# Two mixers of an encoder: the pooled branch's window sums from VectorE to GpSimd

## Chip, cores and metric

The kernel runs on one core of a Trainium2 chip, in one launch. The metric is the device time in microseconds (us) of one execution; less is better. Weights and inputs come from HBM. All arithmetic is float32, and the large products are made from a high and a low part of each operand (float32r), three matmuls for one.

## The reference, cut to what matters

The model has an attention layer, a recurrent layer and then two layers of feed-forward, hybrid mixer, feed-forward. The change touches the hybrid mixer alone, which runs twice (layer 0 and 1). With S = 256 positions and D = 1024:

```python
def causal_pool_mixer(u, pool_w, pool_scale):          # u: [1, 256, 512], 4 groups of 128
    ...
    for g, w in enumerate((2, 4, 8, 16)):              # a window of its own for each group
        lo = jnp.maximum(pos - w, 0)
        window_sum = cs[:, 1:, g] - cs[:, lo, g]
        means.append(window_sum / (pos - lo)[None, :, None])
    mixed = jnp.einsum('bsgc,gcd->bsgd', jnp.stack(means, axis=2) - ug, pool_w)
    return mixed.reshape(b_, s_, 512) * pool_scale

def hybrid_mixer(...):
    u_pool, q_pre, f_pre, i_in, og, gates = jnp.split(h @ w_in, splits, axis=-1)
    pool_out = causal_pool_mixer(u_pool, pool_w, pool_scale)
    ...                                                # a gated linear recurrence over 4 heads: o
    hgrn_out = o * hgrn_norm * jax.nn.silu(og)
    g = jax.nn.sigmoid(gates).reshape(b_, s_, 2, D)
    merged = g[:, :, 0] * (pool_out @ w_pool_proj) + g[:, :, 1] * (hgrn_out @ w_hgrn_proj)
    return merged @ w_out
```

## The kernel before, in words

Channels lie on the 128 partitions and positions along the columns, so a group of the pooled branch is a tile of 128x256. TensorE makes all products. A weight arrives by DMA in a tile `raw`; ScalarE rounds it to `hi` and VectorE makes the rest, `lo` = `raw` - `hi` (`cut`, line 427); activations are split in the same way (`split`, line 473).

The order of the instructions on every engine is written by a planner in the kernel itself. Side work is written as generators (`spawn`), and the planner keeps a modelled clock for each engine (`Clock`, `Engine`). A generator is resumed at the point where TensorE's modelled clock has passed the end of what it last issued, so an instruction's place in TensorE's queue is where the planner expects its operands. For GpSimd its price is 0.1 us and 0.0026 us a column, and 0.12 us for a signal from one instruction to one that needs its result. On the chip each engine takes its queue in order and waits on semaphores.

`hybrid` (line 1472) first makes the products of `h` with `w_in` in pairs of 128 output channels (`pair`), in the order f, q, v, u, og, gates; `scaled` takes each out of PSUM. Beside the later pairs runs `memory`, the linear recurrence: eight levels, each with exponentials on ScalarE (`xx`), two additions (`xx`, `lf`) and two products (`kq`) on VectorE and small matmuls on TensorE. The first six levels' matmuls go into three PSUM tiles `lv`, which `diagonal` masks into `pr` (six levels of 256 columns) and adds up with one reduction. After the levels `memory` normalises the result `ob` and splits it into `hh`, `hl`, the operands of the linear branch.

`pooled` (line 1683) makes the pooled branch. It waits for `u` and for "pool free", which `memory` puts after its last level, since the sums use the buffers of the scan (`lf`, `kk_`, and `ex` as `pd`). Each of four rounds doubles the window for all the groups that are left (one addition, one copy of the first columns), finishes one group (product with 1/count on the first 16 columns, subtraction, scaling with subtraction on the rest), and has TensorE multiply it with `pw`; the result is split into `ph`, `pl`, which the trace calls `hph` and `hpl`. `pd` appears there as `xx`, `up_` with a number behind it.

Then come eight branch products. Each is a pooled half (12 matmuls, from `ph`, `pl`) and a linear half (12 matmuls, from `hh`, `hl`) in one PSUM tile; `merge` multiplies them with the gates. The product with `w_out` follows. PSUM has eight tiles: two `acc` and six `m`; a product takes an `m` where no `acc` is free.

Of the kernel before, what the change touches and what calls it, by code (L numbers as in the profile page):

```python
# [12 lines left out]
ALU = mybir.AluOpType  # L13
AX = mybir.AxisListType
PSUM = bass.MemoryType.PSUM

P = 128
D = 1024
NM = 16
S = 256  # L20
# [99 lines left out]
class Clock:  # L120
# [9 lines left out]
    def range(self, ap):  # L130
        dims = list(ap.ap)
        per = dims[0][0] or 1 << 30
        lo = ap.offset % per
        return ap.tensor.name, lo, lo + 1 + sum((n - 1) * abs(s) for s, n in dims[1:])
# [92 lines left out]
class Builder:  # L227
# [1244 lines left out]
    def hybrid(self, layer, gen):  # L1472
        nc, a = self.nc, self.a
        tt, ts, stt, act, mm = self.tt, self.ts, self.stt, self.act, self.mm
# [5 lines left out]
        hy = self.pool(st, "hy")  # L1480
# [3 lines left out]
        cols = slice(0, S)  # L1484
        big = lambda tag: self.t(hy, [P, H, S], tag)
        fl = lambda t: t.rearrange("p h t -> p (h t)")
        hyb = self.hyb
# [15 lines left out]
        fz, qs = big("fz"), big("qz")  # L1503
        vt = self.t(hy, [P, 2, 512], "vt")
        lf, kk_, w0 = big("lf"), big("kk"), big("w0")
        xx = self.t(hy, [P, 2 * H, S], "xx")
        ex, x2 = xx[:, :H, :], xx[:, H:, :]
        at0 = self.t(hy, [P, H, S], "at0")
        at1 = self.t(hy, [P, H, P], "at1")
        up_, gz = big("up_"), self.t(hy, [P, 16, S], "gz")  # L1510
        ob, og, pd = fz, w0, ex
        pw = self.t(hy, [P, 4, P], "pw")
        pr = self.t(hy, [P, 6, S], "pr")
        hh, hl = self.t(hy, [P, H, S], "hh", F32R), self.t(hy, [P, H, S], "hl", F32R)
        ph, pl = self.t(hy, [P, H, S], "hph", F32R), self.t(hy, [P, H, S], "hpl", F32R)

        def memory():
# [46 lines left out]
            def diagonal():  # L1564

                msk = hyb[:, H_AT["level"][0]:H_AT["level"][0] + 192].rearrange("p (l c) -> p l c", l=6)
                for j in range(3):
                    tt(out=pr[:, 2 * j:2 * j + 2, :].rearrange("p l (g c) -> p l g c", c=32),
                       in0=lv[j].rearrange("p (l g c) -> p l g c", l=2, c=32),
                       in1=msk[:, 2 * j:2 * j + 2, :].unsqueeze(2).to_broadcast([P, 2, 8, 32]), op=ALU.mult)  # L1570
                    self.drop(lv[j])
                    yield "dve"
                blk = (yield from self.grab("work"))[:, :S]
                nc.vector.tensor_reduce(out=blk, in_=pr.rearrange("p l n -> p n l"), axis=AX.X, op=ALU.add)
                yield
                bv = blk.rearrange("p (h j c) -> p h j c", h=H, c=32)
                for q in range(4):
                    p0 = 32 * q
                    nc.scalar.copy(out=at0[p0:p0 + 32, :, p0:p0 + 32], in_=bv[p0:p0 + 32, :, 0, :])
                    nc.scalar.copy(out=at1[p0:p0 + 32, :, p0:p0 + 32], in_=bv[p0:p0 + 32, :, 1, :])  # L1580
                self.put("diag", gen)
# [4 lines left out]
            for i in range(8):  # L1586
# [3 lines left out]
                last = lambda v, h=h: v[:, :, h - 1:h].to_broadcast([P, N // (2 * h), h])  # L1590
# [14 lines left out]
                if i < 5:  # L1605
                    small(i + 1, kq, kq)
                    if i == 4:
                        self.keep(*lv)
                        self.spawn(diagonal(), *lv)
                        up = yield from self.grab("m", 2)  # L1610
                elif i < 7:
                    for hd in range(H):
                        for t0 in range(0, S, 2 * h):
                            j, p0 = t0 // P, t0 % P
                            mm(out=up[j][p0:p0 + h, hd * P + p0 + h:hd * P + p0 + 2 * h],
                               lhsT=kq[:, hd, t0:t0 + h], rhs=kq[:, hd, t0 + h:t0 + 2 * h], start=True, stop=True)
                    yield
                    for j, dst in ((0, at0), (1, at1)):
                        uv = up[j].rearrange("p (h t) -> p h t", h=H)
                        for p0 in range(0, P, 2 * h):  # L1620
                            nc.vector.tensor_copy(out=dst[p0:p0 + h, :, p0 + h:p0 + 2 * h], in_=uv[p0:p0 + h, :, p0 + h:p0 + 2 * h])
                else:
                    ps = up.pop()
                    for hd in range(H):
                        mm(out=ps[:, hd * P:(hd + 1) * P], lhsT=kq[:, hd, 0:P], rhs=kq[:, hd, P:S], start=True, stop=True)
                    yield
                    nc.scalar.copy(out=at0[:, :, P:S], in_=ps.rearrange("p (h t) -> p h t", h=H))
                    self.drop(ps, *up)
                self.drop(kq)
            self.put("pool free", gen)  # L1630
            yield from self.wait("diag", gen)
            yield from self.wait("v", gen)
            sq = yield from self.grab("kq")
            for i in range(2):
                ps = yield from self.grab("m")
# [30 lines left out]
            for i in range(2):  # L1666
                ps = yield from self.grab("m")
# [13 lines left out]
                    self.put("hh", gen, hd)  # L1681

        def pooled():
            yield from self.wait("u", gen, 2)
            yield from self.wait("pool free", gen)
            cur = up_
            for g in range(4):
                wd = 1 << g
                dst = (lf, kk_)[g % 2]
                tt(out=dst[:, g:, wd:], in0=cur[:, g:, wd:], in1=cur[:, g:, 0:S - wd], op=ALU.add)  # L1690
                nc.vector.tensor_copy(out=dst[:, g:, 0:wd], in_=cur[:, g:, 0:wd])
                yield
                i0 = H_AT["inv"][0] + g * NM
                tt(out=pd[:, g, 0:NM], in0=dst[:, g, 0:NM], in1=hyb[:, i0:i0 + NM], op=ALU.mult)
                tt(out=pd[:, g, 0:NM], in0=pd[:, g, 0:NM], in1=up_[:, g, 0:NM], op=ALU.subtract)
                stt(out=pd[:, g, NM:], in0=dst[:, g, NM:], scalar=0.5 / wd, in1=up_[:, g, NM:], op0=ALU.mult, op1=ALU.subtract)
                cur = dst
                yield
                ps = yield from self.grab("m")
                mm(out=ps[:, :S], lhsT=pw[:, g, :], rhs=pd[:, g, :], start=True, stop=True)  # L1700
                yield
                self.split(ps[:, :S], ph[:, g, :], pl[:, g, :], self.v("pool_scale", layer * 4 + g))
                self.drop(ps)
                self.put("ph", gen, g)
# [18 lines left out]
        self.spawn(first(), *pp)  # L1723
        pair(2, fz[:, 2:4, :], ("f2", gen, 0))
        self.spawn(memory())
        for e in (4, 6):
            pair(e, qs[:, e - 4:e - 2, :], ("q", gen, e - 4))
        pv = self.take("acc", 2)
        for c in range(2):
            for half in range(2):  # L1730
                w = self.piece("hi", layer * 2 + c, half)
# [9 lines left out]
        self.drop(*pv)  # L1741
        self.put("v", gen)
        self.spawn(pooled())
        self.spawn(output_gate())
        for c in HYBRID:
            e = 2 * c
            if e < 12:
                dst, name, e0 = up_, "u", 8
            elif e < 16:
                dst, name, e0 = og, "g", 12  # L1750
                self.need("og free", gen)
            else:
                dst, name, e0 = gz, "z", 16
# [14 lines left out]
        def merge(e, ps):  # L1768
            yield from self.wait("gz", gen)
            m0, m1 = [t[:, :S] for t in (yield from self.grab("work", 2))]  # L1770
            stt(out=m0, in0=gz[:, e, :], scalar=1.0, in1=ps[:, 0:S], op0=ALU.add, op1=ALU.mult)
            stt(out=m1, in0=gz[:, 8 + e, :], scalar=1.0, in1=ps[:, S:2 * S], op0=ALU.add, op1=ALU.mult)
            yield
            tt(out=m0, in0=m0, in1=m1, op=ALU.add)
            self.split(m0, mh[:, e, :], ml[:, e, :], 0.5)
            self.put("m", gen, e)

        for e in range(8):
            w = self.piece("wph", layer * 4 + e // 2, e % 2)
            ps = self.take("acc")  # L1780
            self.run(self.prod(ps[:, 0:S], w, e % 2 * 1024, ph, pl, range(4), cols, key=("ph", gen))
                     + self.prod(ps[:, S:2 * S], w, e % 2 * 1024 + 512, hh, hl, range(4), cols, key=("hh", gen), last=True))
            self.spawn(merge(e, ps), ps)
        self.prep(S)

        def residual(d, ps):
# [5 lines left out]
        for d0, n in ((0, 4), (4, 1), (5, 1), (6, 1), (7, 1)):  # L1792
            ps, steps = [], []
            for d in range(d0, d0 + n):
                w = self.piece("hout", layer * 4 + d // 2, d % 2)
# [215 lines left out]
```

## Time and profile before

| | |
|---|---|
| median of 3 runs | 1526.24 us (1525.52 to 1527.98) |
| profiled execution | 1526.28 us, of it 1524.49 us from the first to the last instruction |
| TensorE (PE) busy | 1492.8 us, 98% |
| VectorE (DVE) busy | 1116.3 us, 73% |
| ScalarE (ACT) busy | 903.1 us, 59% |
| GpSimd (POOL) busy | 26.2 us, 2%, 68 instructions |
| mean granted TensorE clock | 0.996 |

Layer 0's mixer lies at about 645 to 800 us of the span, layer 1's at 1170 to 1345 us. In the profile PE is TensorE, DVE VectorE, ACT ScalarE, POOL GpSimd; a granted clock of 1.00 is 2.4 GHz and 0.50 is 1.2 GHz. Almost every instruction bears the line of the planner's helper (L181), so rows are told apart by tile: `lo<-raw,hi` reads `raw` and `hi` and writes `lo`.

### The profile page before, as it was taken

To read this page: it belongs to the slowest core of one execution; us is meant where nothing else is said; L and a number is where in the kernel's file an instruction comes from. 1 tells how busy PE (TensorE), PEld (TensorE's weight loads), DVE (VectorE), ACT (ScalarE), POOL (GpSimd) and SP (SyncE) were. 2 spreads that over 40 slices of the span, in tenths; PEclk is the share of its full clock that TensorE was granted. 3 is DMA by queue.
4 is the path that set the end of the run, shared out by engine and by line. 5 is a ranking of instruction groups with operands and counts; after the bars stand their busy time and mean duration, and the time that the engine had idled before them with its cause. 6 is when DMAs were issued, how large, how long until landed. Compare 5 with 4: busy or idle time off the path is not lost.

```text
span 1524.5 us, 31049 instructions
## 1 busy us (share of the span) xinstructions
PE 1492.8 (98%) x12950; PEld 1458.6 (96%) x12950; DVE 1116.3 (73%) x1882; ACT 903.1 (59%) x1435; POOL 26.2 (2%) x68
## 2 busy tenths in 40 slices
PE   8999999999999999999999999999999998999998
PEld 8988899999999999999999999999999998999998
DVE  6977775689997666669887666666666788877754
ACT  7666654689966654575555554455455754555553
POOL 1000000000000000000000000000000000000000
PEclk9999999999999999999999999999999999999999
DMA  6422224544455555554545655655556444456553
GB/s 239 158 90 84 83 84 141 201 159 168 138 170 190 198 201 172 207 175 146 180 164 186 225 184 177 207 193 197 184 176 227 166 140 138 166 184 223 185 171 123
DMA packets 42492, 259.12 MB, mean 170 GB/s; under 512 B 4840, under 2 KB 6256, under 8 KB 18416
## 3 DMA queue, kind: packets, MB, share of 16 engines
q1 hardware_dynamic: 40624, 251.90, 47.6%
q10 hardware_dynamic: 1728, 5.24, 1.0%
q8 instruction: 101, 1.65, 0.4%
q14 instruction: 39, 0.32, 0.1%
HBM read 256.07 MB, written 1.05 MB: 169 GB/s over the span
## 4 chain that ended last, share of the span: by engine, by line
PE 60%; issue 26%; DVE 8%; ACT 4%; DMA 1%; POOL 1%; SPq 0%; ACTq 0%; DVEq 0%; POOLq 0%
PE acc L181 45%; PE m L181 14%; DVE lo L181 3%; ACT hi L181 2%; DVE big L181 2%; DVE kq L181 1%; ACT w L181 1%; ACT L181 1%; ACT xx L181 1%; DVE xx L181 0%; DVE lf L181 0%; DVE work L181 0%; DMA raw<-in_hin_dram 0%; DMA raw<-in_hi_dram 0%; POOL col L181 0%
## 5 line engine op out<-in xcount | busy, mean ns | idle before, releaser
L181 DVE TENSOR_TENSOR lo<-raw,hi 128x1024 fp32r<-128x1024 f32 (+3 forms) x520 | 582.6, 1129 | 248.0 <-ACT hi L181 243.6
L181 ACT ACTIVATE hi<-raw 128x1024 fp32r<-128x1024 f32 (+3 forms) x520 | 501.5, 980 | 286.7 <-PE acc L181 187.9
L181 PE MATMUL acc<-xh,hi 128*128 128x256 f32 (+1 forms) x2096 | 588.4, 281 | 5.6 <-ACT hi L181 5.6
L181 PE MATMUL acc<-xl,hi 128*128 128x256 f32 (+1 forms) x2096 | 589.0, 281 | 0.0
L181 PE MATMUL acc<-xh,lo 128*128 128x256 f32 (+1 forms) x2096 | 587.4, 280 | 0.0
L181 PEld LDWEIGHTS acc<-xh,hi 128*128 128x128 f32 x2096 | 395.0, 188 | 7.0 <-ACT hi L181 5.6
L181 PEld LDWEIGHTS acc<-xl,hi 128*128 128x128 f32 x2096 | 395.1, 188 | 1.3
L181 PEld LDWEIGHTS acc<-xh,lo 128*128 128x128 f32 x2096 | 394.7, 188 | 1.3 <-DVE lo L181 0.2
L181 PE MATMUL acc<-ph,lo 128*128 128x256 f32 x704 | 194.3, 276 | 0.0
L181 PE MATMUL acc<-ph,hi 128*128 128x256 f32 x704 | 194.3, 276 | 0.0
L181 PE MATMUL acc<-pl,hi 128*128 128x256 f32 x704 | 194.3, 276 | 0.0
L181 PEld LDWEIGHTS acc<-ph,lo 128*128 128x128 f32 x704 | 132.2, 188 | 0.0
L181 PEld LDWEIGHTS acc<-ph,hi 128*128 128x128 f32 x704 | 132.2, 188 | 0.0
L181 PEld LDWEIGHTS acc<-pl,hi 128*128 128x128 f32 x704 | 132.2, 188 | 0.0
L181 PE MATMUL m<-xh,lo 128*128 128x256 f32 (+1 forms) x336 | 95.7, 285 | 0.0
L181 PE MATMUL m<-xl,hi 128*128 128x256 f32 (+1 forms) x336 | 95.5, 284 | 0.0
L181 PE MATMUL m<-xh,hi 128*128 128x256 f32 (+1 forms) x336 | 95.2, 283 | 0.0
L181 DVE TENSOR_TENSOR work<-acc,spread 128x256 f32<-128x256 f32 (+1 forms) x108 | 46.0, 427 | 36.5 <-PE acc L181 32.3
L181 ACT ACTIVATE work<-work 128x256 f32<-128x256 f32 (+2 forms) x92 | 37.4, 408 | 51.7 <-DVE work L181 51.4
L181 PEld LDWEIGHTS m<-xh,hi 128*128 128x128 f32 x336 | 63.7, 190 | 0.2
L181 PEld LDWEIGHTS m<-xh,lo 128*128 128x128 f32 x336 | 63.6, 189 | 0.3
L181 PEld LDWEIGHTS m<-xl,hi 128*128 128x128 f32 x336 | 63.6, 189 | 0.1
(359 smaller groups left out, 2242.2 us busy)
## 6 DMA issues: line engine op xcount, KB each, us to landing
raw<-in_ffn_gu_dram SPq DMA_DIRECT2D x88, 1024.0 KB, 4.9
raw<-in_ffn_dn_dram SPq DMA_DIRECT2D x64, 704.0 KB, 4.1
raw<-in_hin_dram SPq DMA_DIRECT2D x32, 1024.0 KB, 4.9
raw<-in_oin_dram SPq DMA_DIRECT2D x16, 1024.0 KB, 4.9
raw<-in_ein_dram SPq DMA_DIRECT2D x12, 1024.0 KB, 4.8
raw<-in_eout_dram SPq DMA_DIRECT2D x8, 1024.0 KB, 4.9
raw<-in_oout_dram SPq DMA_DIRECT2D x8, 1024.0 KB, 4.9
raw<-in_wph_dram SPq DMA_DIRECT2D x8, 1024.0 KB, 4.9
```

What stands on the lines that cost most here:

```text
L181: r = f(*args, **kw)
```

## The change

Three things in `hybrid`. The window sums go from VectorE to GpSimd: group by group, each from `u` anew, in two tiles `win` of 128x256 of their own, and as soon as `u` is there; "pool free" is gone. A group g makes g+1 additions with as many small copies, a small product, a scaling and a subtraction, then the matmul with `pw` and the split as before. The masked levels are added up pair by pair as they come, so that `pr` has four levels instead of six and the reduction is an addition of two. The pooled halves of the first four branch products are issued before the four linear halves; the other four products are as before.

```diff
-        ob, og, pd = fz, w0, ex
+        ob, og = fz, w0
-        pr = self.t(hy, [P, 6, S], "pr")
+        pr = self.t(hy, [P, 4, S], "pr")
+        win = [self.t(hy, [P, S], f"win{i}") for i in range(2)]
...
                 for j in range(3):
-                    tt(out=pr[:, 2 * j:2 * j + 2, :].rearrange("p l (g c) -> p l g c", c=32),
+                    to = pr[:, 2:4, :] if j else pr[:, 0:2, :]
+                    tt(out=to.rearrange("p l (g c) -> p l g c", c=32),
...
+                    if j:
+                        tt(out=pr[:, 0:2, :], in0=pr[:, 0:2, :], in1=to, op=ALU.add)
                     yield "dve"
                 blk = (yield from self.grab("work"))[:, :S]
-                nc.vector.tensor_reduce(out=blk, in_=pr.rearrange("p l n -> p n l"), axis=AX.X, op=ALU.add)
+                tt(out=blk, in0=pr[:, 0, :], in1=pr[:, 1, :], op=ALU.add)
...
-            self.put("pool free", gen)
...
         def pooled():
+            g_ = nc.gpsimd
             yield from self.wait("u", gen, 2)
-            yield from self.wait("pool free", gen)
-            cur = up_
             for g in range(4):
-                wd = 1 << g
-                dst = (lf, kk_)[g % 2]
-                tt(out=dst[:, g:, wd:], in0=cur[:, g:, wd:], in1=cur[:, g:, 0:S - wd], op=ALU.add)
-                nc.vector.tensor_copy(out=dst[:, g:, 0:wd], in_=cur[:, g:, 0:wd])
-                yield
+                u = cur = up_[:, g, :]
+                for n in range(g + 1):
+                    wd, dst = 1 << n, win[n % 2]
+                    g_.tensor_tensor(out=dst[:, wd:], in0=cur[:, wd:], in1=cur[:, 0:S - wd], op=ALU.add)
+                    g_.tensor_copy(out=dst[:, 0:wd], in_=cur[:, 0:wd])
+                    cur = dst
                 i0 = H_AT["inv"][0] + g * NM
-                tt(out=pd[:, g, 0:NM], in0=dst[:, g, 0:NM], in1=hyb[:, i0:i0 + NM], op=ALU.mult)
-                tt(out=pd[:, g, 0:NM], in0=pd[:, g, 0:NM], in1=up_[:, g, 0:NM], op=ALU.subtract)
-                stt(out=pd[:, g, NM:], in0=dst[:, g, NM:], scalar=0.5 / wd, in1=up_[:, g, NM:], op0=ALU.mult, op1=ALU.subtract)
-                cur = dst
+                g_.tensor_tensor(out=cur[:, 0:NM], in0=cur[:, 0:NM], in1=hyb[:, i0:i0 + NM], op=ALU.mult)
+                g_.tensor_scalar(out=cur[:, NM:], in0=cur[:, NM:], scalar1=0.5 / wd, scalar2=None, op0=ALU.mult)
+                g_.tensor_tensor(out=cur, in0=cur, in1=u, op=ALU.subtract)
                 yield
                 ps = yield from self.grab("m")
-                mm(out=ps[:, :S], lhsT=pw[:, g, :], rhs=pd[:, g, :], start=True, stop=True)
+                mm(out=ps[:, :S], lhsT=pw[:, g, :], rhs=cur, start=True, stop=True)
...
-        for e in range(8):
-            w = self.piece("wph", layer * 4 + e // 2, e % 2)
-            ps = self.take("acc")
-            self.run(self.prod(ps[:, 0:S], w, e % 2 * 1024, ph, pl, range(4), cols, key=("ph", gen))
-                     + self.prod(ps[:, S:2 * S], w, e % 2 * 1024 + 512, hh, hl, range(4), cols, key=("hh", gen), last=True))
-            self.spawn(merge(e, ps), ps)
+        for e0, n in ((0, 4), (4, 1), (5, 1), (6, 1), (7, 1)):
+            pooled_, linear, ps = [], [], []
+            for e in range(e0, e0 + n):
+                w = self.piece("wph", layer * 4 + e // 2, e % 2)
+                ps.append(self.take("acc"))
+                pooled_ += self.prod(ps[-1][:, 0:S], w, e % 2 * 1024, ph, pl, range(4), cols, key=("ph", gen))
+                linear += self.prod(ps[-1][:, S:2 * S], w, e % 2 * 1024 + 512, hh, hl, range(4), cols, key=("hh", gen), last=True)
+            self.run(pooled_ + linear)
+            for i in range(n):
+                self.spawn(merge(e0 + i, ps[i]), ps[i])
```

## Rows read from the trace of the kernel before

**Rows 1.** Busy us by engine in stretches: PE, PEld, DVE, ACT, POOL, granted clock, DMA
```profile
690.00:711.00 21.00, 19.49 (x332) 18.74 (x319) 19.88 (x27) 11.77 (x16) 0.00 (x0) 1.00 0.45 153
711.00:760.00 49.00, 48.59 (x418) 47.80 (x418) 41.63 (x70) 26.61 (x40) 1.64 (x1) 1.00 0.46 154
1210.00:1231.00 21.00, 19.04 (x335) 18.33 (x336) 16.82 (x22) 15.64 (x19) 0.00 (x0) 1.00 0.54 197
1285.00:1291.00 6.00, 2.06 (x8) 1.06 (x8) 5.55 (x15) 1.74 (x4) 0.00 (x0) 0.97 0.22 91
1291.00:1294.00 3.00, 3.00 (x15) 3.00 (x16) 0.69 (x1) 1.99 (x3) 0.00 (x0) 0.50 0.00 0
```

**Rows 2.** Chain of work that ended last, both mixers: start us, us, what
```profile
691.65 1.23 DVE lo L181
...
705.05 1.22 DVE kq L181 x2
...
707.01 12.80 PE acc L181 x111
...
740.29 0.43 PE m L181 x2
...
1252.18 2.93 DVE work L181
```

**Rows 3.** TensorE in order of time, 1284 to 1294 us: start, us, [idle before <-releaser]
```profile
1284.93 0.28 PE L181 MATMUL acc<-hph,hi 128*128 128x256 f32 x1
...
1286.37 0.39 PE L181 MATMUL acc<-hpl,hi 128*128 128x256 f32 x1 [1.16 <-DVE hpl L181]
...
1288.76 0.70 PE L181 MATMUL m<-xx,pw 128*128 128x256 f32 x2 [1.90 <-DVE xx L181]
...
1291.32 0.41 PE L181 MATMUL acc<-hh,hi 128*128 128x256 f32 x1
...
1293.88 0.39 PE L181 MATMUL acc<-hph,hi 128*128 128x256 f32 x1
```

**Rows 4.** VectorE's groups, 1268 to 1292 us: busy us, mean ns | idle before
```profile
L181 DVE SCALAR_TENSOR_TENSOR hpl<-m,vec,hph 128x256 fp32r<-128x256 f32 x4 | 1.9, 478 | 0.8 <-ACT hph L181 0.8
...
L181 DVE TENSOR_TENSOR lf<-up__12257 128x1020 f32<-128x1020 f32 x1 | 1.2, 1216 | 0.0
...
L181 DVE SCALAR_TENSOR_TENSOR xx<-lf,up__12257 128x240 f32<-128x240 f32 x2 | 0.8, 402 | 0.0
```

**Rows 5.** VectorE in order of time, the last part of the linear operand
```profile
1291.03 0.69 DVE L181 TENSOR_TENSOR hl<-fz,hh 128x512 fp32r<-128x512 f32 x1 [0.36 <-ACT hh L181]
```

**Rows 6.** GpSimd and VectorE in order of time, where both work
```profile
36.85 1.11 POOL L181 COPY kz<-kpe 64x272 f32<-64x272 f32 x2 [13.75 <-DVE kpe L181]
37.04 0.65 DVE L181 TENSOR_TENSOR mq<-mq,work 128x272 f32<-128x272 f32 x1
39.48 0.44 DVE L181 TENSOR_TENSOR mq<-mq,work 128x272 f32<-128x272 f32 x1
...
467.07 0.70 POOL L181 TENSOR_TENSOR col<-mx,half 128x2 f32<-128x2 f32 x1 [143.36 <-DVE mx L181]
...
814.68 1.22 DVE L181 TENSOR_TENSOR lo<-raw,hi 128x1024 fp32r<-128x1024 f32 x1
814.85 1.61 POOL L181 TENSOR_TENSOR col<-mx,half 128x2 f32<-128x2 f32 x1 [75.67 <-DVE mx L181]
...
990.01 0.48 DVE L181 TENSOR_SCALAR work<-cst,col 128x128 f32<-128x128 f32 x2 [0.88 <-POOL col L181]
...
1171.59 1.10 DVE L181 TENSOR_SCALAR work<-cst,col 128x128 f32<-128x128 f32 x2
1171.59 0.95 POOL L181 MEMSET at<- 128x1024 f32 x1
```

**Rows 7.** Writers of `u`, layer 0 and 1: ns min/median/max, first and last start
```profile
L181 DVE TENSOR_TENSOR up__6512<-acc,spread x2: 682/683/684, 682.8 to 689.3; 128x512 f32<-128x512 f32 x2
...
L181 DVE TENSOR_TENSOR up__12257<-acc,spread x2: 685/686/687, 1205.4 to 1209.4; 128x512 f32<-128x512 f32 x2
```

## Prediction

> **What bounds the kernel now.** I read the busy time by stretches first. In both mixers there are two kinds of stretch. From 690 to 711 us and from 1210 to 1231 us the queues of VectorE and ScalarE set the pace: VectorE is busy 19.88 and 16.82 of 21 us, TensorE only 19.49 and 19.04, so TensorE idles 1.5 and 2.0 us. From 711 to 760 us TensorE sets it (48.59 of 49 us) [rows 1]. The chain of work that ended last says the same: a level of the scan runs through the weight cut `lo` (1.23 us) and the products `kq` (0.61 us each) on VectorE, and only after 706 us does it pass to TensorE, 111 matmuls in 12.80 us, 0.115 us each [rows 2].
>
> The third kind is the end of the second mixer. From 1285 to 1291 us TensorE has 8 matmuls and VectorE is full; from 1291 to 1294 us the granted clock is 0.50, the lower of TensorE's two levels, 1.2 GHz, after that idle stretch [rows 1]. TensorE stands in the first branch product, waiting for `hpl`, then for the last pooled group, which VectorE makes between other work [rows 3]. Layer 0 has no such hole [rows 1].
>
> **The tail of the second mixer: -6.5 us.** From 1284.93 to 1291.32 us are 6.4 us [rows 3]; in them lie six matmuls of 0.115 and one pool product of 0.43 us [rows 2], 1.1 us, so 5.3 us are lost. The twelve matmuls from 1291.32 to 1293.88 us take 2.56 us at the lower clock [rows 3] instead of 12 x 0.115 = 1.4: 1.2 more. With the pooled branch finished early and 48 pooled matmuls (5.5 us) in front of the first linear half, no wait for `hph` is left. What is late next is `hl`: its last part ends at 1291.72 us [rows 5]. In front of it after 1282 us VectorE loses two `hpl` (0.48 each) and two subtractions (0.40 each) [rows 4], at least 1.8 us, so it comes at 1289.9 us. TensorE would ask for it after 45 more pooled matmuls and six linear ones, 5.9 us past 1284.93 less the pool product of 0.43, at 1290.4 us. So the cover holds; if VectorE were not relieved at all it would cost 1.3 us (bounds -5.2 and -6.5).
>
> **VectorE's window additions, gone.** The first takes 1.22 us, each final subtraction 0.40 [rows 4], some 7 us in a layer with the three smaller additions and the small columns. I book nothing for them beyond the tail: in layer 0 they lie in the stretch where TensorE is full. The work that hides them is TensorE's own; nothing is to be had there.
>
> **The masked levels: -0.4 us.** A reduction of 2.93 us [rows 2] goes; two additions of 128x512 (0.61, as `kq`) and one half as wide (0.4, as the subtraction [rows 4]) come. In layer 1 the reduction lies on the chain: 2.93 - 1.6 = -1.3; I take -1.1. In layer 0 it lies behind the last level, whose matmuls end the chain's VectorE part [rows 2], while the first addition stands in front of that level: +0.7. Bounds -1.3 (nothing lost in layer 0) and +0.7 (nothing gained in layer 1).
>
> **Pool products moved: -3.2 us.** Four of 0.43 us a layer [rows 2] leave the stretches that TensorE fills and go where it idles 1.5 and 2.0 us [rows 1]: -1.7 in layer 0, -1.5 in layer 1 (the tail is counted above). Bounds -3.4 and 0.
>
> **Their splits, moved too: +2.9 us.** Four `hpl` of 0.48 us a layer [rows 4] now stand in VectorE's queue ahead of the cuts and level products that TensorE waits for. Three of four come before the last level of layer 0 (1.4), four at a busy share of 16.82 / 21 in layer 1 (1.5). Bounds 0 and 3.8. ScalarE's `hph` beside them, of like size, hide in its 9 and 5 idle us of each stretch [rows 1]. The DMA of `pw` is issued at the layer's start as before, on the same queue.
>
> **GpSimd beside VectorE: +7.8 us.** A group g makes g+1 steps of an addition and a small copy, then a small product, a scaling and a subtraction: in a layer 14 wide operations with two inputs, 4 wide ones with one, 14 small ones, 32 in all. They start when `u` is written, at 690.0 and 1210.1 us [rows 7], exactly where VectorE sets the pace. No row shows a wide addition on GpSimd. What rows do show is that the two engines hold each other up. A two-column power takes 0.70 us alone and 1.61 us when VectorE has just begun a cut [rows 6]. The other way round, a copy of 272 columns stretches a VectorE product of 0.44 to 0.65 us, by 0.21, and a GpSimd memset beside it makes a pair of scalings take 1.10 instead of 0.48 us, 0.62 more [rows 6]. An addition reads twice what the copy reads: I take 2 x 0.21 = 0.42 us held, 0.21 for a one-input operation, 0.05 for a small one: 14 x 0.42 + 4 x 0.21 + 14 x 0.05 = 7.4 us a layer. Three levels of two cuts and four level products, 3 x (2 x 1.23 + 4 x 0.61) = 14.7 of 21 us [rows 2], read two operands in SBUF, as that stretched product did; so 0.7 of the holds meet one: 5.2 us. VectorE's idle time of 1.1 and 4.2 us [rows 1] absorbs half of itself, since the rest lies inside the chain: 4.7 + 3.1 = 7.8 us. Bounds: 0 (all holds fall into gaps) and 2 x (18 x 0.62 + 14 x 0.1) = 25 us (0.1 for a small one is twice my value; no row has one). A power and a clearing for the linear branch stand behind these on GpSimd's queue, but come 40 us later.
>
> The Trainium skill (SBUF — State Buffer, section "Who interferes with whom") says that whichever of the two engines starts first gets the shared port pair for its whole instruction and the other fully blocks; the rows agree in direction. It speaks against this change. So does the Trainium skill's GPSIMD Engine Reference (section 3.1, "Elementwise — side-by-side cycle accounting"): 2.6 cycles per element for an addition at 1.2 GHz, an estimated 0.55 us for 256 columns, which no row here shows. With 0.55 held instead of 0.42, the sum would be 2.5 us higher.
>
> **The sum** is -6.5 - 0.4 - 3.2 + 2.9 + 7.8 = +0.6 us on the profiled execution's 1526.28 us (span 1524.49 and 1.8 around it; the median of the three runs is 1526.24): **1526.9, say 1527 us**. So a sure gain at one place is paid for by a likely loss at two. The four products' open banks cost nothing that I can see: eight banks, and the merges follow the linear halves as before.
>
> **The rivals.** (A) GpSimd fits into VectorE's gaps, holds 2 us a layer or less: 1526.3 - 6.5 - 0.4 - 3.2 + 2.9 + 0 to 4 = 1519 to 1523 us. For it: 1.1 and 4.2 us of VectorE idle, and operands from PSUM in part of its work; against it: the chain runs through VectorE there. Chance 0.33.
>
> (B) Slower: TensorE stops at the pool products. TensorE takes its queue in order, and each pool product stands where the kernel's own planner expects the group's end. With each of 32 operations waiting for a VectorE operation under way, half of 0.61 to 1.23 us [rows 2] at 0.7, 0.3 us, the chain is 10 us longer than alone. Alone it takes between 18 x 0.53 + 14 x 0.1 = 10.9 us (the copies of [rows 6]: two in 1.11) and twice that for two inputs, 18 us. The planner allows some 19 us: at its price of 0.1 us and 0.0026 us a column, with 0.12 us for each signal, the groups take 2.9, 3.9, 4.8 and 5.8 us, with the products between them. Where the chain passes that, TensorE waits, and behind the waiting product stand the pairs and the level products. From 3 us past the plan this decides; at 4 to 8 us a layer on top of the forecast, of which up to 3 in all are the same time as the holds: 1532 to 1543 us. Chance 0.27. The Trainium skill's exclusive lock (SBUF — State Buffer, section "Who interferes with whom") would bring this about, each alternation costing the loser the rest of a whole instruction.
>
> (C) The change doesn't do what it says at the tail: the linear branch, itself delayed, leaves the hole where it was, another 4 us: about 1531 us. Against it: 1.8 us and more of relief in front of `hl`. Chance 0.04.
>
> **How the numbers follow.** Forecast (1522 to 1531 us) 0.36, A 0.33, B 0.27, C 0.04. Within 0.2% (3 us, about what a measurement of this kernel can tell from no change) I put 0.26, nearly all from the forecast; faster 0.38 (A, and the forecast's lower edge, 0.05), slower 0.36 (B, C, its upper edge, 0.05). The forecast is a mean of two opposed terms, so its own range is 1522 to 1531; for 8 in 10 it must reach A and most of B: **1517 to 1537**.
>
> **What would show it.** Right: no wait for `hph` or `hpl` by TensorE near 1285 us, granted clock 1.00 throughout; `kq` products stretched by 0.2 to 0.5 beside GpSimd rows; TensorE's waits for `kq` longer between `u` and the last level. Rival A: VectorE's durations unchanged there, and the mixers 6 us shorter in layer 1. Rival B: TensorE waiting for the window tiles. Wrong would be a GpSimd addition far from 0.5 us, or waits of TensorE in layer 0 after 711 us, where I expect none.

## Result and profile after

| | before | after |
|---|---|---|
| median | 1527.11 us (4 runs beside it) | 1549.72 us (1547.31 to 1552.3, 4 runs) |
| ratio | | 1.0147, 95% interval 1.0134 to 1.016 |
| span of the profiled execution | 1524.5 us | 1549.0 us |
| mean granted TensorE clock | 0.996 | 0.990 |

The change makes the kernel 22.6 us slower. The forecast was 1527 us, and the range ended at 1537. Of all the executions below one, of e6, took 2129.67 us at a mean granted clock of 0.655; it is left out of e6's median and ratio.

First, where the time is. I cut each mixer at five events: the power of the norm ahead of it, the first product of the scan's result with `v`, the first branch product, the first matmul of the product with `w_out` (its operands are called `mh`, `ml` in the trace), and the power of the next norm. Lengths in us, from the timelines:

| kernel | layer 0: scan, to branch, branch, `w_out` | layer 1: the same |
|---|---|---|
| before | 85.3, 28.5, 21.8, 34.7 | 99.4, 13.9, 29.8, 34.2 |
| after | 90.9, 26.6, 21.8, 44.7 | 106.4, 16.3, 22.1, 43.8 |

The differences are +13.7 us in layer 0 and +11.3 in layer 1; the rest of the kernel differs by -0.4. The last of the four stretches alone is +10.0 and +9.6, and the prediction did not speak of it. The scan is +5.6 and +7.0. A stretch does not always hold the same work: in layer 1, 93 matmuls with `w_in` lie between the scan's result and the first branch product, where before there were 67. These 26 (3.0 us at 0.115) have moved out of the scan.

The page of the kernel after, part 1: busy us by engine, share of the span, instructions.

```profile
PE 1499.9 (97%) x12950; PEld 1465.0 (95%) x12950; DVE 1110.3 (72%) x1846; ACT 901.9 (58%) x1435; POOL 74.6 (5%) x132
```

GpSimd has 64 instructions more, as planned, and 48 us more of work. The busy time by stretches of the kernel after, columns as in [rows 1]; first the two scans beside GpSimd, then the end of the second mixer's linear branch and its branch products, then the start of the `w_out` product in layer 0:

```profile
680.00:713.00 33.00, 26.51 (x471) 24.90 (x471) 28.28 (x38) 15.43 (x23) 23.75 (x33) 1.00 0.33 113
1217.00:1251.00 34.00, 28.79 (x381) 27.32 (x380) 27.27 (x34) 17.67 (x22) 25.24 (x33) 0.90 0.39 135
...
1297.00:1326.00 29.00, 28.96 (x255) 28.79 (x254) 18.58 (x34) 12.87 (x17) 1.67 (x1) 1.00 0.42 146
...
784.00:789.00 5.00, 0.06 (x1) 0.00 (x0) 4.54 (x8) 0.42 (x1) 0.00 (x0) 0.99 0.69 226
789.00:793.00 4.00, 3.96 (x14) 3.33 (x15) 2.48 (x7) 1.48 (x4) 0.00 (x0) 0.50 0.61 242
793.00:803.00 10.00, 10.00 (x79) 10.00 (x78) 2.96 (x5) 2.74 (x3) 0.00 (x0) 0.86 0.01 2
```

Row three answers [rows 1, 3]: the hole that stood at 1285 us is gone, as predicted. Rows four to six are its successor: TensorE issues one matmul in 5 us; then come 4 us at the lower clock (0.50 is 1.2 GHz) with 14 matmuls and 10 us at a mean of 0.86 with 79. At 0.115 us each these 94 take 10.8 us, so 8 of the 19 us are lost to the idle stretch and the clock behind it. In row two, the scan of layer 1, the granted clock is 0.90; three waits for `win`, of 0.99 to 2.52 us, lie in it (next fence).

TensorE of the kernel after in order of time, the longest waits behind 711 us (start, us, [idle before <-releaser]):

```profile
711.83 0.70 PE L181 MATMUL m<-win,pw 128*128 128x256 f32 x2 [1.01 <-POOL win L181]
...
789.04 0.58 PE L181 MATMUL m<-mh,hi 128*128 128x256 f32 x1 [4.98 <-ACT mh L181]
...
1187.25 0.71 PE L181 MATMUL m<-work,cst 128*128 128x128 f32 x4 [2.78 <-DVE work L181]
...
1228.15 0.70 PE L181 MATMUL m<-win,pw 128*128 128x256 f32 x2 [1.71 <-POOL win L181]
...
1241.45 0.70 PE L181 MATMUL m<-win,pw 128*128 128x256 f32 x2 [2.52 <-POOL win L181]
...
1249.90 0.70 PE L181 MATMUL m<-win,pw 128*128 128x256 f32 x2 [0.99 <-POOL win L181]
...
1335.26 0.58 PE L181 MATMUL m<-mh,hi 128*128 128x256 f32 x1 [5.42 <-ACT mh L181]
```

Three kinds of wait are new: for the window tiles `win` (rival B's), for `mh`, the merged branches, and one in the norm ahead of layer 1. The first two belong to different parts of the change, so the experiments take the parts one by one.

### The profile page after: what moved, and what is told of

The parts are those of the page before. It is cut to its first block, busy times and chain, and to the rows that moved or that the text cites. A ratio compares the mean times of both kernels' runs of the same rounds, so it can differ in the third digit from the quotient of the medians.

```text
span 1549.0 us, 31076 instructions
## 1 busy us (share of the span) xinstructions
PE 1499.9 (97%) x12950; PEld 1465.0 (95%) x12950; DVE 1110.3 (72%) x1846; ACT 901.9 (58%) x1435; POOL 74.6 (5%) x132
## 4 chain that ended last, share of the span: by engine, by line
PE 64%; issue 19%; DVE 8%; ACT 3%; DMA 3%; POOL 2%; POOLq 0%; SPq 0%; ACTq 0%; DVEq 0%
PE acc L181 51%; PE m L181 13%; DVE lo L181 3%; DVE big L181 2%; POOL win L181 2%; ACT hi L181 2%; DMA raw<-in_ffn_dn_dram 1%; DVE work L181 1%; DMA raw<-in_hin_dram 1%; DMA raw<-in_ffn_gu_dram 1%; DVE kq L181 0%; ACT w L181 0%; DVE xx L181 0%; POOL col L181 0%; ACT L181 0%
```

## Experiments

All ratios are to the kernel before on the same chip, with 95% intervals.

| run | edit | median, us | ratio |
|---|---|---|---|
| e1_batch_only | before + four pooled halves first | 1542.92 | 1.0098 [1.0081, 1.0116] |
| e2_no_batch | after - four pooled halves first | 1534.83 | 1.0046 [1.0029, 1.0063] |
| e3_levels_only | before + masked levels on the way | 1529.53 | 1.0009 [1.0, 1.0019] |
| e4_late_no_batch | e2, GpSimd behind the last level | 1539.65 | 1.0069 [1.0054, 1.0084] |
| e5_writes_no_batch | e2, GpSimd clears only, no window sums | 1521.76 | 0.9957 [0.9943, 0.9971] |
| e6_price_no_batch | e2, planner's GpSimd price x 2.2 | 1525.81 | 0.9988 [0.9978, 0.9997] |
| e7_vector_no_batch | e2, the same operations on VectorE | 1528.25 | 1.0003 [0.9994, 1.0012] |
| e8_batch2_only | before + two pooled halves first | 1528.08 | 1.0004 [0.9994, 1.0014] |
| e9_split_tiles | e1, pooled weights given back early | 1538.86 | 1.0079 [1.0062, 1.0096] |
| e10_tiles_held | before, four weight tiles held | 1529.05 | 1.0014 [1.0005, 1.0023] |
| e11_price_split | e6 + e9's batch | 1537.25 | 1.0073 [1.0052, 1.0094] |
| e12_price_batch2 | e6 + e8's batch | 1524.76 | 0.9986 [0.9976, 0.9995] |
| e13_batch_each | e1, sums released one by one | 1532.30 | 1.0030 [1.0017, 1.0043] |
| e14_price_each | e6 + e13's batch | 1534.98 | 1.0055 [1.0039, 1.0072] |

### The three parts alone

Each takes one hunk of the diff and leaves the others: e1 the loop of the branch products, e2 the other two, e3 the hunk of `diagonal`.

> The kernel before with one part of the change: the pooled halves of four branch products ahead of their linear halves. Theory 1 (batching holds four pairs of weight tiles and four banks, so the next weights and the gated sums come late and TensorE waits in the product with w_out): TensorE waits 5 us for mh in each mixer, as the changed kernel does near 789 and 1335 us, and runs the next 3 to 4 us at the lower clock; 1537 to 1546 us. Theory 2 (all of the loss is GpSimd beside VectorE in the scan's levels): within 3 us of 1527 us or below, since layer 1's hole is covered by pooled halves.

> The changed kernel with the branch products in the order of before (pooled half, linear half, one product after the other). Theory 1 (batching costs some 10 us in layer 0 and 8 in layer 1, the early sums on GpSimd the rest): 1530 to 1536 us, no wait of 5 us for mh, the level stretches as long as in the changed kernel. Theory 2 (all of it is GpSimd in the levels): 1545 us or more, as the changed kernel.

> The kernel before with the masked levels added up on the way and nothing else. The step of the prediction: -0.4 us with bounds -1.3 and +0.7, so 1526 to 1528 us. If the two additions of 128x512 stand in the scan's chain in both layers: up to +2 us, 1529 us.

The batch alone gives +15 us, the rest of the change +7; together 22, which is the whole loss, so the two barely touch. In e1 the `w_out` stretches are 44.5 and 42.7 us, in e2 34.7 and 34.3, as before: the waits for `mh` belong to the batch. The scans of e2 are 90.9 and 106.6 us, as in the changed kernel. The masked levels alone gain nothing that can be seen.

### The batch of four: weight tiles or late sums

```diff
 # e8_batch2_only: the kernel before with this loop (shown against e1's)
-        for e0, n in ((0, 4), (4, 1), (5, 1), (6, 1), (7, 1)):
+        for e0, n in ((0, 2), (2, 1), (3, 1), (4, 1), (5, 1), (6, 1), (7, 1)):
 # e9_split_tiles: the batch, with the first weight tile of a layer holding four pooled halves, the second four linear ones
+        for half, x_, key, steps in ((0, (ph, pl), "ph", pooled_), (1, (hh, hl), "hh", linear)):
+            for e in range(4):
+                if e % 2 == 0:
+                    w = self.piece("wph", layer * 4 + half, e // 2)
+                steps += self.prod(..., last=e % 2 == 1)
+            self.run(steps)
 # e10_tiles_held: order of before
+        held = [self.piece("wph", layer * 4 + e // 2, e % 2) for e in range(4)]
...
+            if e == 3:
+                self.used(*held)
 # e13_batch_each: four pooled halves, then for each e
+            self.run(self.prod(ps[:, S:2 * S], w, e % 2 * 1024 + 512, hh, hl, ..., last=True))
+            self.spawn(merge(e, ps), ps)
```

> The kernel before with the pooled halves of two branch products first, not four. Theory that four products hold all four pairs of weight tiles, so that the next cuts come in a burst between the gated sums: two hold two, no wait for mh of 5 us, within 2 us of before (1526 to 1530 us). Theory that the loss is only that the gated sums start later by the linear halves put behind: a third of e1's 10 and 8.5 us: 1532 to 1535 us.

> The kernel before with the batch of four alone, and with the weights of the first four branch products laid out another way in DRAM: the first weight tile of a layer holds their four pooled halves, the second their four linear halves, so that TensorE is done with the pooled weights and gives their tiles back before it begins the linear halves. The gated sums start as late as with the batch of four alone (after all four linear halves). If the loss of that run (1.0098) came from the weight tiles all being held, so that eight cuts fell into a burst among the gated sums: TensorE's wait ahead of the w_out product (4.97 us there) is under 1 us, mixer stretches from the first branch product to the w_out product are 35 to 37 us, ratio 1.000 to 1.002. If it came from the four gated sums starting late (VectorE loses some 4 us of time in which the kernel before does them): a wait of 3 to 5 us stays, the stretches are 41 to 44 us, ratio 1.007 to 1.010.

> The kernel before, its branch products in their old order one after the other (each followed by its gated sum), but the weight tiles of the first four are all taken at the start and given back only after the fourth. So the tiles are held as in the batch of four, and the gated sums start as early as before. If held tiles are the cause: the stretch from the first branch product to the w_out product grows from 34.6 to 41 to 45 us, with a wait of 3 to 5 us ahead of the w_out product, ratio 1.007 to 1.010. If late sums are the cause: stretch 35 to 37 us, ratio 1.000 to 1.003.

> The kernel before with the batch of four alone, in the change's order of products and with its weight tiles, but each of the first four gated sums is released as soon as its own linear half is done, not after all four. The first sum then starts some 4 us later than in the kernel before (four pooled halves and one linear half, 5 x 1.35 us, in place of 2 x 1.35) and 4 us earlier than with the batch of four alone (8 x 1.35). If the late sums are the cause: TensorE's wait for mh in the w_out product falls from 4.97 us to under 2, the stretch from the first branch product to the w_out product stays, the one behind it is 35 to 39 us in place of 44.5, ratio 1.000 to 1.004. If the order of the products itself costs (open banks, weights, the burst of cuts): the wait and 1.008 to 1.010 stay.

The batch of four takes all four pairs of `hi` and `lo` tiles at once, so no weight can be cut ahead: that was one theory. The other: the planner releases the four gated sums only when all eight halves are done (10.8 us, against 2.7 for the first one before), and VectorE starts 8 us late. TensorE's first branch matmul and VectorE's first gated product in layer 0, in the kernel before, then after:

```profile
758.39 0.28 PE L181 MATMUL acc<-hph,hi 128*128 128x256 f32 x1
762.33 0.74 DVE L181 SCALAR_TENSOR_TENSOR work<-gz,acc 128x256 f32<-128x256 f32 x2
```

```profile
760.78 0.28 PE L181 MATMUL acc<-hph,hi 128*128 128x256 f32 x1
772.68 0.75 DVE L181 SCALAR_TENSOR_TENSOR work<-gz,acc 128x256 f32<-128x256 f32 x2
```

That is 3.9 us behind the branch matmul before, 11.9 after. e9 frees the tiles and keeps most of the loss; e10 holds them, with early sums, and loses a seventh of it; e13 keeps batch and tiles, starts the sums 4.9 us (layer 0) and 3.9 us (layer 1) earlier than e1, and loses a third. Late sums are the main cause; the tiles account for at most the small rest (e1 against e9, whose sums also start 1.4 us earlier in layer 0; e10's 1.4 per mille).

The rows show why 8 us of lateness decide. ScalarE rounds the fifth, sixth and seventh merged branch (`mh`), and TensorE asks for them; first the kernel before, with TensorE's first `w_out` matmul:

```profile
777.34 0.42 ACT L181 ACTIVATE mh<-work 128x256 fp32r<-128x256 f32 x1 [2.26 <-DVE work L181]
778.58 0.42 ACT L181 ACTIVATE mh<-work 128x256 fp32r<-128x256 f32 x1 [0.83 <-DVE work L181]
784.71 0.42 ACT L181 ACTIVATE mh<-work 128x256 fp32r<-128x256 f32 x1 [2.47 <-DVE work L181]
...
780.15 0.28 PE L181 MATMUL acc<-mh,hi 128*128 128x256 f32 x1
```

The `w_out` product takes the first six merged branches for its first output tile, the sixth of them 15 matmuls or 1.7 us after it starts. In the kernel before the sixth is rounded at 779.0 us and needed at 780.15 + 1.7 = 781.9: 2.9 us to spare; the fifth has 3.8. In the kernel after TensorE already stands at the fifth: it has made 12 matmuls from 782.54 us on and needs it at 783.9, and it is rounded at 789.0. The kernel after, ScalarE's fourth and fifth and VectorE between them:

```profile
779.52 0.42 ACT L181 ACTIVATE mh<-work 128x256 fp32r<-128x256 f32 x1 [0.83 <-DVE work L181]
788.57 0.42 ACT L181 ACTIVATE mh<-work 128x256 fp32r<-128x256 f32 x1 [4.83 <-DVE work L181]
...
780.92 1.23 DVE L181 TENSOR_TENSOR lo<-raw,hi 128x1024 fp32r<-128x1024 f32 x1 [0.53 <-ACT hi L181]
782.07 1.41 DVE L181 SCALAR_TENSOR_TENSOR work<-gz,acc 128x256 f32<-128x256 f32 x4
783.39 1.22 DVE L181 TENSOR_TENSOR lo<-raw,hi 128x1024 fp32r<-128x1024 f32 x1
784.53 0.74 DVE L181 SCALAR_TENSOR_TENSOR work<-gz,m 128x256 f32<-128x256 f32 x2
785.19 2.35 DVE L181 TENSOR_TENSOR lo<-raw,hi 128x1024 fp32r<-128x1024 f32 x2
787.46 0.74 DVE L181 SCALAR_TENSOR_TENSOR work<-gz,m 128x256 f32<-128x256 f32 x2
```

VectorE never idles long: the last sums, which used to lie between the products, now meet the cuts of the next four weights. In e9 and e13 the same first wait of the `w_out` product, TensorE in order of time (first e9, layer 0; then e13, both layers):

```profile
784.20 0.58 PE L181 MATMUL acc<-mh,hi 128*128 128x256 f32 x1 [3.82 <-ACT mh L181]
```

```profile
782.44 0.38 PE L181 MATMUL acc<-mh,hi 128*128 128x256 f32 x1 [1.14 <-ACT mh L181]
...
1322.60 0.38 PE L181 MATMUL m<-mh,hi 128*128 128x256 f32 x1 [1.83 <-ACT mh L181]
```

The wait falls with the lateness: 4.97 us (e1, layer 0), 3.82 (e9), 1.14 and 1.83 (e13), none for `mh` (e8, e10). In e1, e8 and e13 layer 1's old hole is still there (waits of 1.15 for `hpl` and 1.90 for `xx`), since without the early sums the pooled halves, too, are late.

### The early sums on GpSimd

```diff
 # e4_late_no_batch: "pool free" is put and waited for as before
+            self.put("pool free", gen)
+            yield from self.wait("pool free", gen)
 # e5_writes_no_batch: clearings in place of every operation of the sums
-                    g_.tensor_tensor(out=dst[:, wd:], in0=cur[:, wd:], in1=cur[:, 0:S - wd], op=ALU.add)
+                    g_.memset(dst, 0.0)
+                    g_.memset(dst, 0.0)
...
 # e6_price_no_batch: the planner's price
-                ... else 0.1 + 0.0026 * n
+                ... else (0.1 + 0.0026 * n) * (2.2 if op in ("tensor_tensor", "tensor_scalar", "tensor_copy") else 1)
 # e7_vector_no_batch
-            g_ = nc.gpsimd
+            g_ = nc.vector
```

> The changed kernel without the four-product order, and with the window sums on GpSimd only after the last level of the scan, as before. Theory of the lock (GpSimd hurts because it meets the scan's chain on VectorE): the level stretches are back to their length of before, layer 1's hole is smaller since VectorE makes no sums: 1521 to 1526 us. Theory of the wait (GpSimd hurts because its chain is longer than the planner allows and TensorE waits in its queue for the window tiles, wherever they lie): TensorE waits 5 us a layer for win, 1530 us or more.

> As e2 (products in the order of before), but GpSimd makes no window sums: each two-input operation is two clearings of 128x256 (some 0.61 us, as long as a lone addition in the changed kernel), each other one a clearing of its width, so that it writes as much and reads nothing. The window sums are left out. Theory of the shared read path (VectorE's two-operand work and GpSimd's reads hold each other up): kq, xx, lf and lo keep their durations of before beside GpSimd, level stretches 86 and 100 us instead of e2's 90.9 and 106.6, 1521 to 1526 us. Theory that the moved splits and pool products alone cost it: stretches as in e2, 1531 to 1535 us.

> As e2, but the planner reckons 2.2 times as long for additions, scalings and copies on GpSimd, so that TensorE's pool products stand later in its queue. Theory that TensorE's waits for the window tiles are the loss: no waits for win (7.8 us in e2), 1524 to 1528 us. Theory that the holds of VectorE are the loss: waits for win go, but waits for kq stay or grow, level stretches 4 to 6 us above before: 1530 to 1534 us.

> As e2, but the same 32 operations a layer run on VectorE, as soon as u is there. By the rows 14 x 0.42 + 4 x 0.25 + 14 x 0.17 = 9.3 us of VectorE a layer in the stretch that it bounds. If GpSimd spares VectorE most of that: 1537 to 1542 us, clearly above e2. If holding VectorE up costs as much as doing the work on it: within 3 us of e2, 1532 to 1537 us.

GpSimd's operations in the kernel after, in order of time, with VectorE beside them or not:

```profile
683.90 0.82 POOL L181 TENSOR_SCALAR win<-win 128x240 f32<-128x240 f32 x1
...
690.90 1.46 POOL L181 TENSOR_TENSOR win<-win 128x254 f32<-128x254 f32 x1
...
693.70 1.24 POOL L181 TENSOR_SCALAR win<-win 128x240 f32<-128x240 f32 x1
...
695.71 0.61 POOL L181 TENSOR_TENSOR win<-up__6512 128x255 f32<-128x255 f32 x1
696.26 0.18 POOL L181 COPY win<-up__6512 128x1 f32<-128x1 f32 x1
...
1221.86 3.79 POOL L181 TENSOR_TENSOR win<-up__12273 128x255 f32<-128x255 f32 x1 [34.75 <-DVE up__12273 L181]
```

VectorE's groups beside them, 684 to 713 us (busy us, mean ns): first the kernel before, then after, then e5 (680 to 713 us):

```profile
L181 DVE TENSOR_TENSOR xx<-xx,lf 128x512 f32<-128x512 f32 x4 | 2.7, 685 | 0.0
```

```profile
L181 DVE TENSOR_TENSOR lo<-raw,hi 128x1024 fp32r<-128x1024 f32 x6 | 7.5, 1243 | 4.5 <-ACT hi L181 4.5
L181 DVE TENSOR_TENSOR xx<-xx,lf 128x512 f32<-128x512 f32 x4 | 4.5, 1127 | 0.0
L181 DVE TENSOR_TENSOR kq<-xx,qz 128x512 f32<-128x512 f32 x4 | 3.2, 798 | 0.0
L181 DVE TENSOR_TENSOR kq<-xx,kk 128x512 f32<-128x512 f32 x4 | 3.1, 772 | 0.0
```

```profile
L181 DVE TENSOR_TENSOR xx<-xx,lf 128x512 f32<-128x512 f32 x5 | 3.4, 685 | 0.0
L181 DVE TENSOR_TENSOR kq<-xx,qz 128x512 f32<-128x512 f32 x5 | 3.4, 684 | 0.0
```

An addition on GpSimd takes 0.61 us where VectorE leaves it alone, and 0.72 to 1.78 (once 3.79) where not. With 0.61 for each of 10 additions, 0.73 for a subtraction, 0.82 for a scaling and 0.2 for a small one, a layer's 32 operations would take some 15 us; they stretch over 29.8 us in layer 0 and 28.0 in layer 1, waits for TensorE included, and keep GpSimd busy for 23.5 and 25.0 of them. VectorE is held for 4 x 0.44 + 4 x 0.11 + 4 x 0.09 + 6 x 0.02 = 2.7 us in layer 0, and by the same means some 2.1 in layer 1. So the meeting costs GpSimd (8 and 10 us of busy time) several times what it costs VectorE. In e5, where GpSimd only writes, VectorE's additions are at 685 ns again; three of the five `xx` have clearings beside them. (The Trainium skill, SBUF — State Buffer, section "Who interferes with whom", says that a VectorE instruction with two SBUF inputs contends with a GpSimd instruction that reads SBUF and not with one that only writes it. The runs agree: 1127 against 685 ns.)

The planner had priced the chain at some 19 us, and TensorE's window products stood in its queue by that price. With the price raised to 2.2 times (e6) they stand later. Of e2's five waits for `win` of over 0.4 us, 7.8 us together, one is left (1.95 us at 1212 us), and the kernel before is beaten by 0.12% where e2 lost 0.46%: some 9 us for a change that alters no operation. Stretches in us, as in the first table:

| run | layer 0: scan, to branch, branch, `w_out` | layer 1: the same |
|---|---|---|
| e2 | 90.9, 26.6, 21.8, 34.7 | 106.6, 16.3, 24.5, 34.3 |
| e4 | 86.2, 35.4, 21.8, 35.5 | 101.1, 11.2, 36.5, 34.2 |
| e5 | 87.4, 26.6, 21.8, 34.7 | 97.1, 16.6, 26.0, 34.2 |
| e6 | 88.8, 26.4, 21.8, 35.1 | 101.0, 16.4, 26.1, 34.2 |
| e7 | 90.5, 25.7, 21.8, 34.7 | 103.4, 9.5, 30.3, 34.2 |

Not all of the 9 us is the window products. Between the profiled executions of e2 and e6 (8.6 us), 6.1 lie in the two scans behind the first write of `u`, where e2 had lost 10.7 to the kernel before; 1.5 lie in the norm ahead of layer 1 (last section) and 2.8 outside the mixers, and layer 1's branch products give 1.6 back. So more than half of the early sums' loss in the scans was where the planner put four matmuls a layer in an in-order queue. The price also moves the splits behind them, and no run takes the two apart. e6 still lies some 4 to 5 us above e5. The holds, in e6 some 2 us of VectorE in layer 0 and 4 in layer 1, have that size. But e5 does not separate them from the length of the chain: the planner prices its clearings like the operations that they replace, while they keep GpSimd busy for only 11 us a layer, and seven of 46 do not wait for `u`.

e4 moves the sums behind the last level. Its scans are nearly back at their length of before (86.2 and 101.1 us), but it is the slowest of the runs with the order of before: the chain ends too late for its consumers. TensorE in order of time, e4:

```profile
756.82 0.70 PE L181 MATMUL m<-win,pw 128*128 128x256 f32 x2 [3.06 <-POOL win L181]
...
1302.78 1.22 PE L181 MATMUL m<-win,pw 128*128 128x256 f32 x2 [5.15 <-POOL win L181]
```

e7 contradicted both of my expectations: 32 operations a layer, early, on the engine that I had called full cost nothing against fewer and wider ones late (1.0003). Its scans are 5.2 and 4.1 us longer than before, but most of that is matmuls that now fall there: four pool products a layer (1.7 us), and 9 and 25 matmuls with `w_in` (1.0 and 2.9 us) that used to lie behind the scan's result. So the added VectorE work costs TensorE some 2.4 us in layer 0 and nothing visible in layer 1: the scan has more slack on VectorE than its busy share suggests.

### The parts put together again

e11, e12 and e14 are e6 with the batches of e9, e8 and e13.

> The changed kernel with the planner's GpSimd price times 2.2 and with the batch of four in the layout that gives the pooled weights back early. If held tiles are the cause of the batch's loss, the batch now only covers the hole at the tail of layer 1 (waits for hpl and xx, some 3 us): 1519 to 1525 us, ratio 0.994 to 0.998. If late sums are the cause: 1538 to 1544 us, ratio 1.007 to 1.010.

> The changed kernel with the planner's GpSimd price times 2.2 and a batch of two branch products in place of four. The batch of two alone neither lost nor gained on the kernel before (1.0004), and the price alone gave 0.9988. Both theories of the batch: 1523 to 1528 us, ratio 0.997 to 1.000; a gain over the price alone only if the two pooled halves (2.7 us) cover part of the waits for hpl and xx at the tail of layer 1.

> The changed kernel with the planner's GpSimd price times 2.2 and with the batch of four whose gated sums are released one by one. If late sums are the cause of the batch's loss: 1522 to 1530 us, ratio 0.997 to 1.002 (the price alone gave 0.9988; the waits of 1.6 us for hh and hl at the tail of layer 1 go, and what is left of the late sums comes on top). If the order itself costs: 1538 to 1544 us.

e11 keeps the batch's loss. e12 is the fastest complete kernel here, 2.2 us under the kernel before by the medians, and within its interval no better than e6. e14 missed: I expected 1522 to 1530 us and got 1535. Its layer 0 behaves like e13's (`w_out` 37.8 us); layer 1 does not. ScalarE, then VectorE, then TensorE of e14 in order of time:

```profile
1301.11 1.04 ACT L181 ACTIVATE gz<-gz 128x1024 f32<-128x1024 f32 x1
...
1304.27 0.75 DVE L181 SCALAR_TENSOR_TENSOR work<-gz,acc 128x256 f32<-128x256 f32 x2
...
1320.64 0.58 PE L181 MATMUL m<-mh,hi 128*128 128x256 f32 x1 [5.40 <-ACT mh L181]
```

There the gates `gz` themselves are ready only at 1302.15 us, 10.8 us behind the first branch product, so all four sums start together behind them, whatever releases them, and the wait is back at 5.40 us. In the kernel after the gates are ready just as late (10.8 us), so in its layer 1 the late release is not the only cause. Covering the hole also brings the `w_out` product to 11.3 us behind the gates, where before it came 16.2 us behind them. The batch covers the tail's hole (first branch product to `w_out` 22.1 us, e6 26.1) and the `w_out` stretch pays it back twice (43.2 us, e6 34.2).

## Why the prediction was wrong

**The step that failed** is one sentence: "The four products' open banks cost nothing that I can see: eight banks, and the merges follow the linear halves as before." The merges do follow the linear halves, but the first linear half now follows four pooled ones. Of the 24.5 us between the two profiled executions, 19.6 lie in the `w_out` stretches (10.0 + 9.6), so all the rest together came to some +5 us, 2.4 of them in the norm ahead of layer 1, where the sum had +0.6. I had counted banks, and not asked who reads what the moved products make: the sums on VectorE, then the rounding on ScalarE, then a product that needs the fifth and sixth of eight sums 1.4 and 1.7 us after it starts, with 3.8 and 2.9 us to spare. The term should have been a rival at the least: with 12 x 0.115 = 1.4 us for a half, three more pooled halves ahead of the first linear one are 4.1 us, and releasing the first sum only behind the fourth linear half is as much again. In layer 1 the gates, too, come late for a `w_out` product that starts earlier (e14).

**The tail of layer 1: right, then lost.** No wait for `hph` or `hpl` is left and the clock there is 1.00. From the scan's result to the `w_out` product layer 1 gains 43.67 - 38.32 = 5.3 us in the changed kernel, although 3.0 us of `w_in` matmuls have moved in: 8.3 us for the same work, against 6.5 for the hole and 1.5 for the pool products. 2.9 of the 5.3 come from the early sums alone (e2). But a hole covered by pooled matmuls leaves VectorE's sums where they were, and the hole moved to `mh`.

**Pool products moved: half right.** The stretch to the branch products of layer 0 loses 1.8 us (forecast 1.7). But the four products did not go into idle time: they lengthen the scan by their 1.7 us, where TensorE's idle time did not shrink but grew, from 2.8 to 7.0 us. So the -1.7 of layer 0 did not come.

**The masked levels: not shown to be off.** e3 measured +1.4 us, interval 0 to +2.9, for -0.4 forecast with an upper bound of +0.7; the interval reaches into the bounds.

**GpSimd beside VectorE: the sum about right, its parts not, so partly luck.** From the first write of `u` to the scan's result, layer 0 grows by 5.8 us and layer 1 by 4.6, or 7.6 with the matmuls that moved out: 13.4 us, of which 3.4 are the pool products. The other 10.0 stand against 7.8 + 2.9 = 10.7 forecast for holds and splits. (The sums began behind the first write of `u`, at 682.0 us in layer 0, not at 690.0 as the prediction had put them.) But 5.2 us of holds a layer were forecast, and 2.7 and 2.1 measured. In layer 0 TensorE's four waits for `kq` grew from 1.03, 0.48, 0.59 and 0.44 us to 1.62, 1.09, 1.23 and 1.29, by 2.7 us, which is just the holds; with the wait of 1.01 for `win` and the four pool products of 0.43 that moved in, that is 5.4 of the scan's +5.6. In layer 1 the waits for `kq` before the last level went and those for `win` came (5.2 us after): there rival B, with a chance of 0.27, is what happened, and by its mechanism: the chain passed the 19 us of the plan by 9 us, and TensorE stood at the window products. B's own time, 1532 to 1543 us, holds e2's 1534.83. So without the batch the range would have held the time, though not the forecast.

**What was asked of the profile** decided well for the parts that had been thought of: `kq` stretched by 0.09 to 0.11 us rather than 0.2 to 0.5, `xx` by 0.44, the window tiles waited for. "Waits of TensorE in layer 0 after 711 us" stood under what would be wrong, and the one of 4.98 us at 789 is it. So did a GpSimd addition far from 0.5 us: alone it takes 0.61, but nine of the twenty took 0.72 us or more.

## What to carry to other kernels

When products are reordered so that one operand has more time, follow what each product feeds, down to the next product: what is made from it may have three microseconds to spare, and a hole covered at one end can open at the other and cost the lower clock besides. When work goes to an engine that shares something with a busy one, price it as it runs beside that engine (here 23 to 25 us busy in place of some 15), above all where a planner turns the price into a place in an in-order queue: correcting the price was worth some 9 us here, while the move itself won 2 at the end. Take a change of three parts apart before judging it; here two of them together were worth 0.1% once priced rightly, and the third alone made two thirds of the loss.

## What the runs showed of the hardware

The norm ahead of layer 1 met GpSimd's clearings in another phase. VectorE and GpSimd of the kernel after, in order of time:

```profile
1184.89 2.36 DVE L181 TENSOR_SCALAR work<-cst,col 128x128 f32<-128x128 f32 x2 [0.59 <-POOL col L181]
...
1184.81 0.95 POOL L181 MEMSET xx<- 128x1024 f32 x1
1185.70 1.41 POOL L181 MEMSET at<- 128x1024 f32 x2
```

The stretch behind it, columns as in [rows 1]:

```profile
1188.00:1195.00 7.00, 7.00 (x49) 7.00 (x48) 4.29 (x6) 3.95 (x5) 0.00 (x0) 0.76 0.50 175
```

A pair of scalings that takes 0.48 us alone, and took 1.10 beside one clearing [rows 6], ends here only with the clearings, after 2.36 us, and TensorE waits 2.78 us for it; the granted clock of the next 7 us is 0.76. Nothing in the change touches these instructions; their time shifted by what came earlier. Clearings thus held up these scalings, while e5's clearings left two-input additions at 685 ns. The size of this effect differs from run to run of the table (TensorE's wait is under 0.4 us before and in e6, 0.67 in e7 and 2.44 in e2). From the norm's power to the first write of `u` layer 1 takes 35.3 us before, 36.1 in e6, 37.7 in e2 and 37.8 after, so it puts up to 2.4 us into a comparison here that the edits do not explain.
